# Gates' stage of a decoder block: low parts of weights on VectorE, a new order of its first products, and attention's results added up in DRAM by DMA

## The chip, the cores and the metric

One core of one Trainium2 chip runs the whole layer in one launch. The metric is the device time of one execution in microseconds (us); the time of a kernel is the median of its runs. Five engines have queues of their own: TensorE (PE, with its weight loads as PEld), VectorE (DVE), ScalarE (ACT), GpSimd (POOL) and SyncE (SP, which here only starts DMA transfers).

## What is computed

One decoder layer on 2048 tokens of width 1024, in float32. A projection gives pool channels, queries, keys, values and two gates; a causal pooling mixer and a sliding-window attention (window 128, 16 query heads of 64 on 2 key/value heads, a learned sink) run side by side; the gated sum goes through an output projection, and a convolutional gated MLP (width 2816) follows. Cut to what matters here:

```python
h = rmsnorm(x, attn_norm[l])
z = h @ w_in[l]                       # pool | q | k | v | gate_pool | gate_attn
gates = sigmoid(z[..., o4:] + b_gate[l])
g_pool, g_attn = gates[..., :D_MODEL], gates[..., D_MODEL:]
a = pool_mixer(u_pool, w_pool[l], pool_scale[l])
b = swa_sink_attention(q, k, v, sinks[l])
x = x + (g_pool * a + g_attn * b) @ w_out[l]
h = rmsnorm(x, ffn_norm[l])
up = causal_depthwise_conv(h @ w_up[l], conv_w[l], conv_b[l])
x = x + (silu(gate) * val) @ w_down[l]
```

## The kernel before

The tokens are worked in two chunks of 1024 (`T`). A float32 matrix product is made of three products of a reduced format: each operand is split into a high part (a copy in the reduced format) and a low part (operand less high part), and high·high, high·low and low·high are summed in PSUM. Weights therefore pass through a raw tile "R" (3 buffers) into a tile "U" (19 buffers) with both parts. `split` makes the low part by a subtraction on VectorE. `split_added` (L235 to L237) makes it without VectorE: ScalarE copies the high part (L235), ScalarE writes minus the high part into the low part (L236: the raw tile times −1, in the reduced format), and a DMA that GpSimd starts (L237) adds the raw tile to it in SBUF.

Each chunk goes through these stages: keys and values; attention; gates; output projection (`out_proj`); `up`; `down`. Attention is 32 items, 4 groups of heads (`q4` 3, 2, 1, 0) by 8 blocks of 128 queries. An item has `scores` (L863, then mask, maximum and exponentials on VectorE and ScalarE, L872 to L888), `probabilities` (transposes on TensorE, L896, and a select on GpSimd, L904) and `values` (L924). Between them TensorE runs `fillers`: products of the query, pool and gate projections that `fillers(c, group)` lists block by block. `values` copies each 64-partition half of its PSUM result to the other half of a tile (L934, ScalarE) and adds the two key/value halves (L935, VectorE) into a tile of 1 MB per group of heads; three of the four are stored into the DRAM tensor `tad`, the fourth (`q4` 3) stays in SBUF for the gates of the columns 6 and 7, which are fillers.

The other six column tiles of the gates are the gates' stage: six units (`Gates`, columns 4, 5, 2, 3, 0, 1), each a two-by-two block product done with seven products of 12 matmuls of 128x512 (L1161): `one` (A11·B11), `two` (A12·B21), `three` (S2·T2), `four` (S1·T1), `five` (S3·T3), `six` (S4·B22) and `seven` (A22·T4). B are quarters of the normalized input, T sums of them (`right_t1` to `right_t4`, from input tiles loaded and scaled by `scaled_input`, L1386); A are quarters of the unit's weights, S sums of them (L373 to L385, VectorE) out of the two raw tiles `w_ga` and `w_gp`. Each unit's `Blocks.step` makes such a part and splits it: three tiles of 128x1024 a unit by `halved` (with `split_added` for the gates, by L356 and L357 for `up`). `kept` (L1179) copies a product from PSUM, L1191 to L1209 add products up, `value` and `gate` (L1354 to L1365) apply the sigmoids and multiply by what `Gates.fetch` loads from `tad` (attention) and `dd` (pooling).

`Stream` hands out weights in a fixed order: at each `get` the raw tiles of the next two entries are loaded, and the next entry is split ahead. Within each engine, a scheduler sets the order of the instructions; each engine's queue then runs in that order, waiting on semaphores.

Of the kernel before, what the change touches and what calls it, by code (L numbers as in the profile page):

```python
# [26 lines left out]
P = 128  # L27
D = 1024
S = 2048
T = 1024  # L30
# [45 lines left out]
class Stream:  # L76
# [61 lines left out]
def fillers(c, i):  # L138

    q = queries_of(0) + queries_of(1)  # L140
    g = gates_of(0)
    pu = [pooled_of(j) for j in range(4)]
    if i == 3:
        out = [[f] for f in g[6:] + pu[3] + [("one", 0, 0), ("two", 0, 0)]]
        out[4].insert(0, ("gates", 0, 0))
        return out
    fold = [("fold", j, 0) for j in FOLDS[FOLD_FIRST:] if c == 0 and i == 0]
    out = fold + (q[:4] + pu[0][2:] + q[4:6], q[6:] + pu[1][:2] + g[:2] + pu[1][2:],
                  pu[2][:2] + g[2:6] + pu[2][2:])[i]
    return [out[n * len(out) // NB:(n + 1) * len(out) // NB] for n in range(NB)]  # L150
# [13 lines left out]
def weight_order():  # L164
    out = []
    for c in range(NCH):
        if c > 0:
            out.append(("kv",))
        else:
            out += [("fold", j) for j in FOLDS[:FOLD_LEAD]]  # L170
        out += [(kind, j) for parts in first_fillers(c) for kind, j, n in parts if n == 0]
        for i in range(4):
            out += [(kind, j) for parts in fillers(c, i) for kind, j, h in parts
                    if h == 0 and kind not in ("one", "two")]
        out += [("gates", i) for i in range(1, len(UNITS))]
# [27 lines left out]
def block_kernel(ctx: ExitStack, tc: tile.TileContext, x, xT, pos, vec, qkn, w_poolT, w_pool, w_q, w_kv,  # L203
# [29 lines left out]
    def split_added(hi, lo, src):  # L233

        A.copy(hi, src)  # L235
        A.activation(lo, src, AF.Copy, scale=-1.0)  # L236
        G.dma_start(lo, src.bitcast(F32R), accum_op=ALU.add)  # L237
# [51 lines left out]
    def split_weights(key, raws):  # L289
        if key[0] in ("up", "gates"):  # L290
            return Blocks(raws, key[0] == "gates")
# [8 lines left out]
        for raw in raws:  # L300
# [4 lines left out]
            if key[0] in ("ga", "pg", "pu") or key[0] == "q" and key[1] < 4:  # L305
                split_added(hi, lo, raw)
# [26 lines left out]
    class Blocks:  # L333
# [6 lines left out]
        def __init__(self, raws, added=False):  # L340
            self.raws, self.w, self.at, self.added = raws, {}, 0, added
# [8 lines left out]
        def halved(self, first, second, raw):  # L350
            t = up_.tile([P, 2, 8, P], F32R, "U")
            self.tiles.append(t)
            if self.added:
                split_added(t[:, 0], t[:, 1], raw)
            else:
                A.copy(t[:, 0], raw)  # L356
                V.tensor_sub(t[:, 1], raw, t[:, 0].bitcast(F32))  # L357
# [478 lines left out]

    def load_queries(it):
# [73 lines left out]
    def values(it):  # L911
# [15 lines left out]
        ob = qp.tile([P, 2, P], F32, "Q")  # L927
        pe = pv.rearrange("p (c e) q -> p e c q", e=2)
        if it["q4"] not in it["ta"]:
            it["ta"][it["q4"]] = up_.tile([P, 2, T], F32, "U")  # L930
        tt = it["ta"][it["q4"]][:, :, n * P:(n + 1) * P]
        for e in range(2):
            own, other = slice(64 * e, 64 * e + 64), slice(64 - 64 * e, 128 - 64 * e)
            A.copy(ob[own], pe[other, e])  # L934
            V.tensor_add(tt[own], pe[own, e], ob[own])  # L935


    tad, dd, xd = (dp.tile([8, P, T], F32, n) for n in ("tad", "dd", "xd"))

    def pair_of(t, j):  # L940
        return t[2 * j:2 * j + 2].rearrange("k p t -> p k t")
# [395 lines left out]
    class Gates(Up):  # L1337


        def __init__(self, c, ct, b):  # L1340
            super().__init__(c, ct, b, None)

        def halo(self, m):
            return fp.tile([P, 2 + T], F32, "F")

# [34 lines left out]
    def scaled_input(c, j):  # L1380
# [3 lines left out]
             .rearrange("(k p) t -> p k t", p=P))  # L1384
        for k in range(2):
            A.activation(t[:, k], t[:, k], AF.Identity,  # L1386
                         scale=vc[:, V_AN + 2 * j + k:V_AN + 2 * j + k + 1])
        return t

    def gates(c, units, b, xg, last_probabilities, last_values):  # L1390
# [21 lines left out]
        u0.four()  # L1412
        right_t3(xg, b)
        u0.three()
        weights(1, 2)
        u1.four("a")
# [3 lines left out]
        u0.six()  # L1420
# [3 lines left out]
        u1.three()  # L1424
        u0.gate()
        weights(2, 2)
        u1.five()
# [184 lines left out]
    def mixer(c, hs, kvw):  # L1612
# [48 lines left out]
        def done(it):  # L1661
            values(it)
            if it["n"] == NB - 1 and it["q4"] < 3:
                load(pair_of(tad, it["q4"]), ta[it["q4"]])

        xg = []
        for i in range(len(items)):
# [4 lines left out]
            if i > 1:  # L1672
                done(items[i - 2])
# [9 lines left out]
            if units[0].w:  # L1683
                units[0].w.step(1)
            if i == len(items) - 2:
                run_later(9)
                xg = [scaled_input(c, j) for j in (0, 1)]
        done(items[-2])
        run_later(9)
        return gates(c, units, b, xg, lambda: probabilities(items[-1]), lambda: done(items[-1]))  # L1690
# [105 lines left out]
```

## Time and profile before

| | before |
|---|---|
| median of 3 runs | 2505.67 us (2501.68 to 2507.39) |
| profiled execution, its own time | 2498.63 us |
| its span | 2496.9 us |
| mean granted clock of TensorE | 0.989 |
| gates' stage of chunk 0 | 385 to 546 us |
| gates' stage of chunk 1 | 1608 to 1768 us |

The profile is one execution. Its rows name the line, the engine, the operation, and the tiles as output<-input with buffer numbers left out. A row "[1.67 <-POOL M L904]" says that the engine was idle for 1.67 us before this group, until line 904 on GpSimd had written a tile M. `U<-R` stands for the accumulating DMA of L237.

### The profile page before, as it was taken

To read this page: it belongs to the slowest core of one execution; us is meant where nothing else is said; L and a number is where in the kernel's file an instruction comes from. 1 tells how busy PE (TensorE), PEld (TensorE's weight loads), DVE (VectorE), ACT (ScalarE), POOL (GpSimd) and SP (SyncE) were. 2 spreads that over 40 slices of the span, in tenths; PEclk is the share of its full clock that TensorE was granted. 3 is DMA by queue.
4 is the path that set the end of the run, shared out by engine and by line. 5 is a ranking of instruction groups with operands and counts; after the bars stand their busy time and mean duration, and the time that the engine had idled before them with its cause. 6 is when DMAs were issued, how large, how long until landed. Compare 5 with 4: busy or idle time off the path is not lost.

```text
span 2496.9 us, 30624 instructions
## 1 busy us (share of the span) xinstructions
PE 2403.2 (96%) x11108; PEld 1977.8 (79%) x11108; DVE 1898.7 (76%) x2994; ACT 1254.9 (50%) x2279; POOL 204.1 (8%) x154
## 2 busy tenths in 40 slices
PE   8999997988999999999999999988999999999999
PEld 7877875767888888878888888766788888888887
DVE  8577877566887777799955878855669777779994
ACT  6556556554555555543522544654545455554432
POOL 0123221100000000000002131211000000000000
PEclk9999999999999999999999999999999999999999
DMA  9677666879432233455234454478662222227321
GB/s 349 199 233 216 212 194 176 208 221 325 173 101 76 81 122 101 139 198 196 92 143 151 146 173 143 151 181 219 224 228 84 94 76 77 95 74 278 127 77 51
DMA packets 161912, 399.74 MB, mean 160 GB/s; under 512 B 14433, under 2 KB 50785, under 8 KB 153825
## 3 DMA queue, kind: packets, MB, share of 16 engines
q1 hardware_dynamic: 153840, 370.33, 43.6%
q0 software_dynamic: 7488, 27.27, 6.0%
q8 instruction: 87, 1.43, 0.2%
q14 instruction: 65, 0.52, 0.1%
q10 hardware_dynamic: 432, 0.19, 0.0%
HBM read 255.78 MB, written 114.69 MB: 148 GB/s over the span
## 4 chain that ended last, share of the span: by engine, by line
PE 78%; DVE 7%; DMA 6%; ACT 4%; issue 4%; POOL 0%; SPq 0%; DVEq 0%; ACTq 0%; POOLq 0%
PE f L1161 20%; PE f L252 18%; PE t L1161 12%; PE a L1161 6%; PE f L1593 4%; PE a L1593 4%; PE s L1593 4%; PE t L1593 4%; DMA U<-R 2%; PE a L924 1%; PE s L863 1%; PE a L252 1%; ACT Q L882 1%; PE t L896 1%; DMA R<-w_gp 1%
## 5 line engine op out<-in xcount | busy, mean ns | idle before, releaser
L252 PE MATMUL f<-U,U 128*128 128x512 f32 (+1 forms) x2784 | 652.3, 390 | 13.7 <-ACT U L229 5.4
L252 PEld LDWEIGHTS f<-U,U 128*128 128x128 f32 x2784 | 511.0, 189 | 122.8 <-ACT U L229 7.2
L1161 PE MATMUL f<-U,U 128*128 128x512 f32 x1872 | 456.6, 395 | 18.1 <-ACT Q L1179 9.0
L1161 PEld LDWEIGHTS f<-U,U 128*128 128x128 f32 x1872 | 354.7, 191 | 101.0 <-ACT Q L1179 13.8
L1161 PE MATMUL t<-U,U 128*128 128x512 f32 x1392 | 339.4, 397 | 16.2 <-DMA U<-R 13.8
L1227 DVE SCALAR_TENSOR_TENSOR M<-F,vc,M 128x1024 f32<-128x1024 f32 x176 | 225.2, 1282 | 140.8 <-ACT M L1224 140.5
L1161 PEld LDWEIGHTS t<-U,U 128*128 128x128 f32 x1392 | 265.2, 191 | 77.0 <-DMA U<-R 16.3
L1161 PE MATMUL a<-U,U 128*128 128x512 f32 x768 | 187.3, 390 | 2.9 <-DMA U<-R 2.9
L1161 PEld LDWEIGHTS a<-U,U 128*128 128x128 f32 x768 | 143.7, 188 | 33.6 <-DMA U<-R 3.7
L356 ACT CAST U<-R 128x1024 fp32r<-128x1024 f32 x120 | 125.4, 1053 | 62.6 <-DVE R L385 31.1
L1161 PE MATMUL f<-U,M 128*128 128x512 f32 x624 | 151.5, 390 | 2.1 <-DVE F L1205 2.1
L357 DVE TENSOR_TENSOR U<-R,U 128x1024 fp32r<-128x1024 f32 x120 | 146.5, 1222 | 0.0
L882 ACT ACTIVATE Q<-s,st,rq 128x128 f32<-128x128 f32 x256 | 114.0, 455 | 60.8 <-DVE st L879 58.6
L1161 PEld LDWEIGHTS f<-U,M 128*128 128x128 f32 x624 | 116.7, 188 | 27.9 <-DVE F L1205 3.6
L1213 ACT COPY F<-f 128x512 f32<-128x512 f32 x52 | 30.5, 587 | 189.7 <-PE f L1161 189.7
L1551 ACT CAST U<-U 128x1024 fp32r<-128x1024 f32 x76 | 79.0, 1051 | 84.4 <-PE s L1593 21.5
L904 POOL TENSOR_SCALAR_AFFINE_SELECT M<-M 128x1024 fp32r<-128x1024 f32 x64 | 93.6, 1463 | 334.3 <-DVE st L884 205.5
L1224 ACT ACTIVATE M<-F,vc 128x1024 f32<-128x1024 f32 x88 | 109.4, 1243 | 2.0 <-DVE F L1209 0.5
L1552 DVE TENSOR_TENSOR U<-U,U 128x1024 fp32r<-128x1024 f32 x76 | 92.0, 1219 | 3.9 <-ACT U L1551 3.8
L1551 ACT CAST F<-U 128x1024 fp32r<-128x1024 f32 x44 | 46.2, 1050 | 92.0 <-PE a L1593 53.7
L1179 ACT COPY Q<-f 128x512 f32<-128x512 f32 x104 | 61.0, 586 | 51.0 <-PE f L1161 50.9
L924 PE MATMUL a<-M,U 128*128 128x512 f32 x240 | 73.2, 411 | 13.4 <-POOL M L904 5.3
(281 smaller groups left out, 3877.8 us busy)
## 6 DMA issues: line engine op xcount, KB each, us to landing
R<-w_up SPq DMA_DIRECT2D x80, 512.0 KB, 3.8
U<-R POOLq DMA_DIRECT2D x52, 512.0 KB, 5.4
actd<-M SPq DMA_DIRECT2D x44, 512.0 KB, 2.7
U<-w_down SPq DMA_DIRECT2D x88, 256.0 KB, 5.2
U<-actd SPq DMA_DIRECT2D x88, 256.0 KB, 5.3
qd<-U SPq DMA_DIRECT2D x64, 256.0 KB, 3.8
Q<-qd SPq DMA_DIRECT2D x64, 256.0 KB, 4.1
R<-w_out SPq DMA_DIRECT2D x32, 512.0 KB, 5.0
```

The lines of the kernel that those rows point to most:

```text
L252: nc.tensor.matmul(out, a, b, start=(i == 0), stop=(i == n - 1))
L356: A.copy(t[:, 0], raw)
L357: V.tensor_sub(t[:, 1], raw, t[:, 0].bitcast(F32))
L882: A.activation(pr[:, h, :], sc[:, h, 0:P], AF.Exp, bias=nm[:, h:h + 1], scale=it["rq"][:, h:h + 1], accum_out=rs[:, h:h + 1])
L904: G.affine_select(own.rearrange("p a h q -> p (a h) q"), pa.bitcast(F32).rearrange("p a h q -> p (a h) q"), pattern=[[0, 8], [1, P]], base ...
L924: nc.tensor.matmul(pv, v, p[:, a], start=(i == 0), stop=(i == 2 * len(todo) - 1))
L1161: nc.tensor.matmul(bank, a[:, x, k, :], b[k // 2][:, y, k % 2, :], start=(first and i == 0), stop=(i == 11), skip_group_check=True)
L1224: A.activation(y, u[:, 2:], AF.Identity, bias=cw[:, 3, m:m + 1], scale=cw[:, 2, m:m + 1])
L1227: V.scalar_tensor_tensor(y, u[:, j:j + T], cw[:, j, m:m + 1], y, op0=ALU.mult, op1=ALU.add)
L1551: A.copy(hi, src)
L1552: V.tensor_sub(lo, src, hi.bitcast(F32))
L1593: nc.tensor.matmul(into[m], u[:, 0, c_], v[:, 1], start=(first and j == 0), stop=(k == n - 1 and j == 2), skip_group_check=True)
```

## The change

1. `halved` splits the gates' weights as those of `up`: a copy on ScalarE and a subtraction on VectorE. 36 uses of `split_added` go; 16 remain (queries, pool and gate projections), and their DMA now reads the weights in DRAM instead of the raw tile in SBUF.
2. `values` copies the whole PSUM result (128x512) once into a tile of 4 blocks. After every fourth block SyncE stores the first 64 partitions into `tad`, and GpSimd starts a DMA that adds the other 64 partitions to it in DRAM. For `q4` 3 the sum is loaded back (1 MB).
3. Fillers of the last group of heads: block 6 gets `one` and `two` of unit 0, block 7 those of unit 1 (before: unit 0's one after the other in blocks 6 and 7; unit 1's after attention). The weights of units 0 and 1 and the first input tiles are fetched, split and scaled at stated blocks.
4. In `gates`, `two` of unit 2, `four` of unit 0 and its S4·B22 (a new `early`; `six` then only adds) stand ahead of the sums T2, and unit 1's likewise ahead of T3.
5. At the gates' last entry the stream doesn't split the first `w_out` entry ahead; it is split together with the second at the end of `gates`.

```diff
-        if later is None:
+        if key[0] == "gates" and self.entries[i + 1][0] == "out":
+            pass
+        elif later is None:
             self.part(i + 2)
...
-        out = [[f] for f in g[6:] + pu[3] + [("one", 0, 0), ("two", 0, 0)]]
-        out[4].insert(0, ("gates", 0, 0))
-        return out
+        out = [[f] for f in g[6:] + pu[3]]
+        out[3].insert(0, ("gates", 0, 0))
+        out[5].insert(0, ("gates", 1, 0))
+        return out + [[("one", i, 0), ("two", i, 0)] for i in range(2)]
...
-    def split_added(hi, lo, src):
+    def split_added(hi, lo, src, again):
         A.copy(hi, src)
         A.activation(lo, src, AF.Copy, scale=-1.0)
-        G.dma_start(lo, src.bitcast(F32R), accum_op=ALU.add)
+        G.dma_start(lo, again.bitcast(F32R), accum_op=ALU.add)
...
-            if self.added:
-                split_added(t[:, 0], t[:, 1], raw)
-            else:
-                A.copy(t[:, 0], raw)
-                V.tensor_sub(t[:, 1], raw, t[:, 0].bitcast(F32))
+            A.copy(t[:, 0], raw)
+            V.tensor_sub(t[:, 1], raw, t[:, 0].bitcast(F32))
...
-        for e in range(2):
-            own, other = slice(64 * e, 64 * e + 64), slice(64 - 64 * e, 128 - 64 * e)
-            A.copy(ob[own], pe[other, e])
-            V.tensor_add(tt[own], pe[own, e], ob[own])
+        key = it["q4"], n // 4
+        if n % 4 == 0:
+            it["ta"][key] = up_.tile([P, 4, 512], F32, "U")
+        t = it["ta"][key]
+        A.copy(t[:, :, n % 4 * P:n % 4 * P + P], pv)
+        if n % 4 == 3:
+            c_ = slice(n // 4 * 512, n // 4 * 512 + 512)
+            dst = tad[2 * key[0]:2 * key[0] + 2, :, c_].rearrange("c (e d) t -> d (c e) t", e=2)
+            load(dst, t[0:64])
+            G.dma_start(dst, t[64:P], accum_op=ALU.add)
+            if key == (3, 1):
+                it["ta"][3] = up_.tile([P, 2, T], F32, "U")
+                load(it["ta"][3], pair_of(tad, 3))
...
+        def early(self):
+            self.mul(self.z, "S4", "B22")
+            self.z_done = True
...
         u0, u1, u2 = units[:3]
-        weights(1, 1)
-        u1.one()
+        weights(2, 1)
+        u2.one("t")
         last_probabilities()
         weights(1, 1)
-        u1.two()
-        weights(2, 1)
-        right_t1(xg, b, None)
-        u2.one("t")
+        u2.two()
         last_values()
-        xg += [scaled_input(c, j) for j in (2, 3)]
-        u2.two()
+        xg += [load_input(c, j) for j in (2, 3)]
+        u0.four()
+        u0.early()
+        weights(1, 2)
+        for j in (2, 3):
+            scale_input(xg[j], j)
         t2s = right_t2(xg, b, None)
-        u0.four()
+        u1.four("a")
+        u1.early()
         right_t3(xg, b)
         u0.three()
-        weights(1, 2)
-        u1.four("a")
+        u0.six()
         u0.five()
...
+            if group == 3:
+                if 3 <= n < 7:
+                    units[0].w.step(1)
+                if n == 5:
+                    run_later(9)
+                    units[1].w.step(1)
+                    xg.append(load_input(c, 0))
+                if n == 6:
+                    scale_input(xg[0], 0)
+                    xg.append(load_input(c, 1))
+                if n == 7:
+                    scale_input(xg[1], 1)
...
+        right_t1(xg, b, None)
```

TensorE's order at the end of attention in chunk 0, before the change. `a_... <-M` of L924 are values of a block, `t_... <-identr` of L896 its transposes; of the L1161 products, `f_4155` and `a_4185` are `one` and `two` of unit 1, `t_4216` and `a_4250` those of unit 2, `t_4274` is `four` of unit 0:

```order
L896 MATMUL t_4170<-identr_91,Q_4086 128x128 x4
L1161 MATMUL f_4155<-U_353,U_4150 128x512 x2
L1161 MATMUL a_4185<-U_363,U_4150 128x512 x2
L924 MATMUL a_4231<-M_4175,U_452 128x512 x2
L924 MATMUL a_4231<-M_4178,U_453 128x512 x2
L1161 MATMUL f_4155<-U_353,U_4150 128x512 x4
L1161 MATMUL f_4155<-U_358,U_4150 128x512 x6
L1161 MATMUL a_4185<-U_363,U_4150 128x512 x4
L1161 MATMUL a_4185<-U_368,U_4150 128x512 x6
L1161 MATMUL t_4216<-U_353,U_4203 128x512 x2
L1161 MATMUL t_4274<-U_4208,U_4132 128x512 x4
```

And the same place after it (lines moved by 3 to 5). `t_4090` and `a_4120` are `one` and `two` of unit 2, `t_4146` is `four` of unit 0 and then its S4·B22 (the rows with U_888 and U_893), while `a_4195`, next below these rows, the same of unit 1:

```order
L929 MATMUL a_4068<-M_4050,U_453 128x512 x2
L1164 MATMUL t_4090<-U_353,U_4086 128x512 x4
L1164 MATMUL t_4090<-U_358,U_4086 128x512 x6
L901 MATMUL t_4105<-identr_91,Q_4010 128x128 x4
L1164 MATMUL a_4120<-U_363,U_4086 128x512 x6
L1164 MATMUL a_4120<-U_368,U_4086 128x512 x6
L929 MATMUL a_4134<-M_4110,U_452 128x512 x2
L929 MATMUL a_4134<-M_4113,U_453 128x512 x2
L1164 MATMUL t_4146<-U_4075,U_3990 128x512 x6
L1164 MATMUL t_4146<-U_4079,U_3990 128x512 x6
L1164 MATMUL t_4146<-U_888,U_3990 128x512 x6
L1164 MATMUL t_4146<-U_893,U_3990 128x512 x6
```

Unit 1's `one` and `two` now stand before these rows, between scores, transposes and values of the last blocks, and 48 products without T2 to T4 follow the last values.

GpSimd's order in chunk 0 after the change, over about two groups of four blocks (L909 is the select, L240 the DMA of `split_added`, L941 the adding DMA of `values`):

```order
L909 AFFINE_SELECT M_3254<-M_3251 128x1024
L941 DMA tad_208<-U_3003 64x4x512
L909 AFFINE_SELECT M_3324<-M_3321 128x1024
L240 DMA U_3389<-w_gp 128x1024
L240 DMA U_3545<-wfold_84 128x1024
L909 AFFINE_SELECT M_3401<-M_3398 128x1024
L909 AFFINE_SELECT M_3472<-M_3469 128x1024
L909 AFFINE_SELECT M_3560<-M_3557 128x1024
L941 DMA tad_208<-U_3313 64x4x512
```

Each L941 stands between the selects of two blocks, behind the store of the same tile on SyncE's queue; before the change there were only selects and the DMAs of L237.

More of the change, by code (lines that the diff above doesn't have):

```diff
@@ L174, in weight_order @@
                     if h == 0 and kind not in ("one", "two")]
-        out += [("gates", i) for i in range(1, len(UNITS))]
+        out += [("gates", i) for i in range(2, len(UNITS))]
         out += [("out", m) for n in range(2) for m in range(KT)]
@@ L835, in rotate, with pair_of @@
         V.tensor_add(x[h, 1], x[h, 1], t[h, 0])
+    tad, dd, xd = (dp.tile([8, P, T], F32, n) for n in ("tad", "dd", "xd"))
+    def pair_of(t, j):
+        return t[2 * j:2 * j + 2].rearrange("k p t -> p k t")
     def load_queries(it):
@@ L1423, in gates @@
         weights(2, 1)
-        u1.three()
+        u1.six()
+        u1.five()
         u0.gate()
-        weights(2, 2)
-        u1.five()
+        weights(2, 1)
         n = len(units)
```

47 lines of the change are left out of this document (20 added, 27 removed).

## The prediction

> **What bounds the kernel now.** I read the page first, then busy times by stage, then TensorE's idle places in the gates' stage, then the waits there. The page's first part:
>
> ```profile
> span 2496.9 us, 30624 instructions
> PE 2403.2 (96%) x11108; PEld 1977.8 (79%) x11108; DVE 1898.7 (76%) x2994; ACT 1254.9 (50%) x2279; POOL 204.1 (8%) x154
> ```
>
> TensorE (PE) is busy 96% of the span; 2496.9 − 2403.2 = 93.7 us are idle. Its products are the same in number before and after, so the change can win only that idle time and what slow clock costs. Busy times by stage (start:end, length, then busy of PE, PEld, DVE, ACT, POOL, then granted clock, DMA share, GB/s):
>
> ```profile
> 130.00:385.00 255.00, 241.93 (x1225) 201.25 (x1224) 205.76 (x441) 142.44 (x414) 65.93 (x46) 0.99 0.71 213
> 385.00:546.00 161.00, 133.48 (x538) 102.40 (x537) 99.39 (x127) 89.99 (x126) 19.48 (x20) 0.94 0.71 192
> 546.00:660.00 114.00, 106.70 (x473) 85.99 (x472) 79.28 (x107) 57.26 (x90) 2.44 (x2) 0.99 0.83 295
> 1060.00:1284.00 224.00, 222.06 (x974) 181.60 (x973) 201.14 (x284) 93.94 (x112) 0.00 (x0) 1.00 0.48 164
> 1348.00:1608.00 260.00, 258.56 (x1341) 218.23 (x1341) 208.51 (x432) 119.97 (x392) 66.29 (x34) 1.00 0.47 157
> 1608.00:1768.00 160.00, 134.60 (x539) 103.34 (x538) 98.81 (x125) 89.52 (x127) 19.26 (x20) 0.94 0.71 191
> ```
>
> The second and the last rows are the gates' stage of the two chunks. TensorE is idle there for 27.5 and 25.4 us, 53 of the 94 us, and no engine is full: VectorE (DVE) has 99 of 161 us. The clock is 0.94 against 1.00 elsewhere; 6% of 161 us is about 9.7 us a chunk. So idle time and clock hold 37 and 35 us, **72 us in all, the most that the stage can give**. Attention in chunk 1 (row 1348) has 1.4 us idle in 260, so what the change saves there on other engines is hidden. Attention in chunk 0 has 13 us idle and out_proj (row 546) 7 us.
>
> The idle places of chunk 0 in TensorE's timeline (start, length, group, idle before it and what ended it):
>
> ```profile
> 391.09 0.73 PE L924 MATMUL a<-M,U 128*128 128x512 f32 x2 [1.67 <-POOL M L904]
> 394.24 0.63 PE L896 MATMUL t<-identr,Q 128*128 128x128 f32 x4 [1.47 <-DVE Q L888]
> 400.06 1.20 PE L924 MATMUL a<-M,U 128*128 128x512 f32 x4 [2.36 <-DVE F L1191]
> 404.72 0.50 PE L924 MATMUL a<-M,U 128*128 128x512 f32 x1 [1.15 <-ACT M L898]
> 407.00 1.22 PE L924 MATMUL a<-M,U 128*128 128x512 f32 x2 [1.05 <-POOL M L904]
> 410.20 3.91 PE L1161 MATMUL f<-U,U 128*128 128x512 f32 x10 [1.99 <-DMA U<-R]
> 419.95 2.56 PE L1161 MATMUL t<-U,U 128*128 128x512 f32 x10 [1.75 <-DMA U<-R]
> 429.21 0.50 PE L1161 MATMUL f<-U,U 128*128 128x512 f32 x1 [2.39 <-ACT U L1036]
> 445.16 2.57 PE L1161 MATMUL a<-U,U 128*128 128x512 f32 x10 [1.48 <-DMA U<-R]
> 456.21 1.43 PE L1161 MATMUL t<-U,U 128*128 128x512 f32 x5 [1.00 <-DMA U<-R]
> 471.08 2.88 PE L1161 MATMUL a<-U,U 128*128 128x512 f32 x12
> 473.80 2.88 PE L1161 MATMUL t<-U,M 128*128 128x512 f32 x12
> 509.02 7.17 PE L1161 MATMUL f<-U,U 128*128 128x512 f32 x24 [3.61 <-ACT Q L1179]
> 527.66 7.59 PE L1161 MATMUL t<-U,U 128*128 128x512 f32 x22 [4.31 <-DMA U<-R]
> ```
>
> Three kinds. **Attention's tail**, 388 to 410: the five quoted gaps are 7.7 us (the window's unquoted gaps are under 1 us each). **Waits for a low part that comes by accumulating DMA** (`U<-R`): 1.99 + 1.75 + 1.48 + 1.00 + 4.31 = 10.5 us, and the 3.61 us at 509 stand behind such a transfer in the chain of waits, as does the last gap:
>
> ```profile
> 505.98 5.05 DMA U<-R
> 519.41 8.20 DMA U<-R
> ```
>
> **The input's split**, 2.39 us at 429 and some gaps near 1 us. Twelve products back to back take 473.80 − 471.08 = 2.72 us, 0.227 each; at 527 twenty-two take 7.59, 0.345 each: the slow clock after a long gap.
>
> **Part 1: low parts on VectorE.** What a step costs now and then:
>
> ```profile
> L357 DVE TENSOR_TENSOR U<-R,U 128x1024 fp32r<-128x1024 f32 x120 | 146.5, 1222 | 0.0
> L236 ACT ACTIVATE U<-R 128x1024 fp32r<-128x1024 f32 x52 | 55.0, 1058 | 0.1
> L237 POOL DMA_DIRECT2D U<-R x52 | 45.4, 873 | 275.5 <-ACT U L236 113.2 <-DVE U L1037 43.0 <-DVE R L377 29.8
> U<-R POOLq DMA_DIRECT2D x52, 512.0 KB, 5.4
> POOL U L237 <- ACT U L236: 35.5, 8, 10.9
> ```
>
> Of 52 steps, 36 (6 units, 3 tiles, 2 chunks) are the gates'. Each loses 1.06 us of ScalarE, 0.87 of GpSimd (POOL) and 5.4 of transfer behind the cast, 7.3 us of latency, and gets one subtraction of 1.22 us. VectorE takes on 36 × 1.22 = 44 us, 18 subtractions a chunk; four of them now run inside attention, 14 × 1.22 = 17 us in the stage. 99 + 17 = 116 us of VectorE against some 122 of products (538 × 0.227). Six units share them, 19.4 us each, and a unit's 84 products take 19.0. Row 1060 shows VectorE at 201 of 224 us, 90%, with TensorE at 99%, so this can be carried if the order is kind; 116/0.9 = 129 us. I count all ten-odd microseconds of `U<-R` gaps and the 3.6 behind one as gone: **−14 us a chunk**. What is late next is the raw weights on which the sums are formed, and VectorE itself. The wait that remains, in the stage of chunk 0:
>
> ```profile
> DVE R L376 <- DMA R<-w_gp: 9.8, 2, 5.7
> ```
>
> Up to 5.7 us at once, hidden behind products now. With no slack on VectorE some of it leaks: I take **+3 us**, between 0 and 9.8, nearer to 0 because the stage's first part, attention's last blocks and the input's sums, holds more than its share of the 116.
>
> **Part 2: order.** The last two blocks of attention carried 12 products each beside them (2.7 us, the row at 471); now 24 each, and right after it 24 products of S1·T1 with S4·B22, which need only two tiles of the input's T1 and one of B22, are followed by 24 of the next unit's. Some 30 us of products lie ahead of the first that needs T4, and by adding durations in the new order VectorE has about as much to do in that time. Attention's tail shrinks but doesn't vanish: two blocks gain 2 × 2.7 us of cover against 7.7 us of gaps: **−5 us**. The 2.4 us at 429 and the like are partly covered: **−1.5**.
>
> New waits: the second input tile is loaded one block later and its scaling stands ahead of the last blocks' exponentials on ScalarE. Loads of this size and their neighbours, us to landing last:
>
> ```profile
> U<-xT SPq DMA_DIRECT2D x8, 1024.0 KB, 8.6
> tad<-U SPq DMA_DIRECT2D x6, 1024.0 KB, 4.9
> M<-tad SPq DMA_DIRECT2D x12, 512.0 KB, 6.2
> U<-made_ga SPq DMA_DIRECT2D x2, 1024.0 KB, 10.7
> ```
>
> An 8.6 us landing against a block of some 8 us leaves 2 to 3 us of ScalarE waiting, of which TensorE sees up to that: I take **+2.5** (0 to 8.6, the whole landing).
>
> **Part 3: out's first split later.** The first weight of out_proj is no longer split while the last gates run; the first two now come together at the stage's end: four casts and four subtractions of half the size of L357's, about 0.6 us each, 2.4 us on either engine, in front of out_proj's first product. By the order some 50 products, 11 us, cover them, so **+1** (0 to 4.8).
>
> **Part 4: results added in DRAM.** Per block two copies of 0.37 us and two additions of 0.42 go, one copy of 128x512 comes:
>
> ```profile
> L934 ACT COPY Q<-a 64x256 f32<-64x256 f32 x128 | 47.1, 368 | 50.0 <-DVE U L935 47.7
> L935 DVE TENSOR_TENSOR U<-a,Q 64x256 f32<-64x256 f32 x128 | 53.5, 418 | 28.3 <-ACT Q L934 26.0
> L1179 ACT COPY Q<-f 128x512 f32<-128x512 f32 x104 | 61.0, 586 | 51.0 <-PE f L1161 50.9
> ```
>
> ScalarE saves 0.74 − 0.59 = 0.15 us a block, VectorE 0.84, 53.5 us over 64 blocks. Attention hides nearly all of it (1.4 us idle in chunk 1); it pays for Part 1's 44 us in the sum of VectorE. In chunk 0 there are 13 idle us to win, by fewer accumulates into SBUF and raw buffers that come free sooner; I take **−2**, once (−13 to +10). The price: 16 stores and 16 accumulating DMAs of 512 KB for 6 stores of 1 MB, and two loads of 1 MB. Behind each accumulate, which must wait for its store, GpSimd's selects queue (the order above), and behind SyncE's load of the sums in chunk 1 `made_ga` queues. Nothing before accumulates in DRAM; a store of 1 MB lands in 4.9, an accumulate in 5.4. A block has 8 us between selects, so one is hidden where it comes out of step; I take **+1.5 a chunk**, from 0 to 8 × 4.9 = 39.
>
> **Clock.** Fewer gaps, less slow clock: of 9.7 us about 6.5 come back, by the share of the gaps that goes (about two thirds): **−6.5**.
>
> Sum a chunk: −14 − 5 − 1.5 − 6.5 + 3 + 2.5 + 1 + 1.5 = **−19**; twice that and the −2 of chunk 0 make −40. The profiled execution took 2498.6 us (span 2496.9 and 1.7 around it); it would become 2459. The median of the runs is 2505.7, 7 above it; taken off the median, **2466 us**.
>
> A rule is weighed here. Selects on GpSimd, alone and beside a VectorE operation:
>
> ```profile
> 248.90 2.03 POOL L904 TENSOR_SCALAR_AFFINE_SELECT M<-M 128x1024 fp32r<-128x1024 f32 x1 [8.04 <-DVE st L884]
> 257.52 1.08 POOL L904 TENSOR_SCALAR_AFFINE_SELECT M<-M 128x1024 fp32r<-128x1024 f32 x1 [5.77 <-DVE st L884]
> ```
>
> One is 0.95 us longer. By the Trainium skill, "SBUF — State Buffer", section "Who interferes with whom", a VectorE instruction with two SBUF inputs and a GpSimd instruction that reads SBUF exclude each other, which speaks against Part 1, as its subtractions read two tiles. The trace's 0.95 us agrees. By it the four subtractions a chunk that fall into attention would cost at most 8 × 0.95 = 8 us, −32 for −40; without it nothing. The sum goes without, as attention's selects have slack.
>
> **Rivals.**
> *VectorE becomes the bound.* For it: 116 us against 122 of products, chains in which each waits for the other. At 81% of its time (205.8 of 255 in chunk 0's attention) the stage takes 143 us, 18 less than now, −36; at 75%, 155, −12. Against it: row 1060's 90%. I put it at −20: 2486.
> *The stage runs nearly gapless.* All of the new waits hidden and 4 us left of 36 a chunk: −64, 2442. Against it: attention's last block, whose probabilities and values form one chain over four engines.
> *The accumulates hold attention up (slower).* Each of the 16 keeps GpSimd for a store's landing, 4.9 us, with a select behind it that the next values need. At 16 × 4.9 = 78 less the 40, +38: 2544. It decides from 40/16 = 2.5 us each not hidden. Against it: a block's 8 us and GpSimd busy only 66 of 255 us.
> *It moves the stalls only.* out_proj of chunk 0 has a DMA share of 0.83 and waits for weights now; arriving 20 us earlier it may wait that much longer, and chunk 1 likewise: 2501 to 2508.
>
> **How the numbers follow.** Forecast 0.50 (2453 to 2478), VectorE the bound 0.20 (2478 to 2500), gapless 0.15 (2434 to 2453), stalls moved 0.07, slower by accumulates 0.08. The range 2438 to 2499 leaves out a fifth of the gapless case, 0.03, a little of the second, 0.01, and the last two, 0.15. Within 0.2% (2500.7 to 2510.7, about what a measurement of this kernel can tell from no change) lie the moved stalls: 0.07; slower 0.08; faster 0.85.
>
> **What would show it.** Part 1: no `U<-R` gaps on TensorE in the stage, the stage at about 140 us, VectorE at 115 in it, clock 0.97 or more. Part 2: gaps between the last blocks of 4 us or less. Part 3: under 2 us idle at out_proj's start. Part 4: accumulates landing within 6 us, no select behind one that TensorE waits for. Wrong it would be if attention grew by more than 5 us in a chunk, or TensorE waited for VectorE's subtractions or for raw weights by more than 10.

## The result, and the profile after

| | before | after |
|---|---|---|
| median | 2503.68 us (4 runs, 2497.79 to 2507.39) | 2440.24 us (4 runs; three of them 2438.13 to 2440.7) |
| ratio | | 0.9746, 95% interval 0.972 to 0.9772 |
| profiled execution, its span | 2498.63, 2496.9 us | 2440.7, 2439.0 us |
| mean granted clock | 0.989 | 0.994 |

The change made the kernel 63 us faster by the medians, 58 by the two profiles (2498.6 and 2440.7). One of the four runs after took 3567.56 us, at a granted clock of 0.619; it counts in that median and in nothing else here. The first part of the page after:

```profile
span 2439.0 us, 30309 instructions
PE 2383.8 (98%) x11108; PEld 1973.2 (81%) x11108; DVE 1888.0 (77%) x2902; ACT 1205.1 (49%) x2179; POOL 192.3 (8%) x134
```

TensorE's idle time is 55 us in place of 94, and its busy time, for the same 11108 instructions, 19 us less. The granted clock rose with it, from 0.989 to 0.994 as a mean over the span, which by itself would be some 12 of the 19 us. To see where the time went I cut both kernels at the same three events in TensorE's timeline: the first scores of a chunk, the first scores of its last group of heads (for short, the last group), and the first product of out_proj. Out_proj's own stretch is counted from there to the transposes of L635 in the norm that follows; 20 us of its products come after them, in both kernels. Busy times by these stretches, before (chunk 0 twice, then chunk 1; columns as in the prediction):

```profile
130.00:337.00 207.00, 193.93 (x976) 160.43 (x975) 164.15 (x351) 117.05 (x334) 55.88 (x38) 0.98 0.74 222
337.00:546.00 209.00, 181.48 (x787) 143.22 (x786) 141.00 (x216) 115.38 (x205) 29.53 (x28) 0.95 0.68 188
1366.00:1558.40 192.40, 190.96 (x993) 160.96 (x992) 162.12 (x337) 93.18 (x309) 45.27 (x25) 1.00 0.44 149
1558.40:1767.60 209.20, 183.80 (x798) 145.21 (x798) 140.32 (x210) 113.58 (x204) 29.41 (x27) 0.95 0.66 186
```

And after:

```profile
130.00:325.60 195.60, 190.63 (x975) 159.56 (x974) 148.83 (x307) 110.90 (x312) 61.04 (x43) 0.99 0.88 243
325.60:509.80 184.20, 173.79 (x787) 140.99 (x786) 150.18 (x212) 95.73 (x176) 18.41 (x13) 0.98 0.61 184
1332.20:1524.50 192.30, 190.64 (x991) 160.92 (x990) 146.25 (x293) 87.23 (x287) 50.94 (x30) 1.00 0.61 180
1524.50:1708.20 183.70, 174.47 (x797) 142.74 (x796) 149.81 (x206) 93.89 (x174) 18.39 (x12) 0.98 0.51 158
```

Last group to out_proj: 209.2 to 184.2 and 209.1 to 183.7 us, −25 in each chunk. Attention up to the last group: −11 in chunk 0, nothing in chunk 1. Out_proj up to L635: 79.1 to 81.4 and 69.6 to 71.5 us, +2 each. That is −11 − 25 − 25.4 + 2.3 + 1.9 = −57.2 of the 57.9 us between the spans. The same three numbers are given below for each experiment.

TensorE's gaps after, last blocks and gates of chunk 0:

```profile
386.54 1.22 PE L868 MATMUL s<-U,Q 128*128 128x256 f32 x8 [2.19 <-ACT Q L887]
396.28 0.73 PE L929 MATMUL a<-M,U 128*128 128x512 f32 x2 [1.65 <-POOL M L909]
403.72 0.74 PE L929 MATMUL a<-M,U 128*128 128x512 f32 x2 [0.76 <-POOL M L909]
407.91 3.02 PE L1164 MATMUL t<-U,U 128*128 128x512 f32 x12 [0.68 <-ACT Q L1182]
412.34 2.56 PE L1164 MATMUL a<-U,U 128*128 128x512 f32 x10 [0.50 <-DVE U L357]
419.00 4.41 PE L1164 MATMUL a<-U,U 128*128 128x512 f32 x12 [2.51 <-ACT Q L1182]
506.97 3.02 PE L1164 MATMUL f<-U,M 128*128 128x512 f32 x12 [1.15 <-DVE F L1208]
```

No `U<-R` is left among them, and between 419 and 507 TensorE has no gap of over 0.15 us. The longest gap is 2.51 us at 419, behind a copy out of PSUM on ScalarE. The waits in the same place of chunk 1 tell why:

```profile
ACT U L1039 <- DMA tad<-U: 4.8, 1, 4.8
PE a L1164 <- ACT Q L1182: 2.8, 1, 2.8
...
1614.00:1624.00 10.00, 7.28 (x25) 5.78 (x26) 6.35 (x7) 4.63 (x6) 0.00 (x0) 0.83 0.23 90
```

(The letters PE, ACT and DMA name who waits for what; then us in all, times, longest. The last row has the columns of the stretches above.) ScalarE wants to write a split of the input (L1039) into the U buffer that the last attention results leave, and waits 4.8 us until their accumulate into `tad` has landed; the copy of PSUM stands behind it in ScalarE's order, and TensorE behind that. In the 10 us around this gap the granted clock is 0.83.

### The profile page after: what moved, and what is told of

It is laid out like the page before. It is cut to its first block, busy times and chain, and to the rows that moved or that the text cites. A ratio compares the mean times of both kernels' runs of the same rounds, so it can differ in the third digit from the quotient of the medians.

```text
span 2439.0 us, 30309 instructions
## 1 busy us (share of the span) xinstructions
PE 2383.8 (98%) x11108; PEld 1973.2 (81%) x11108; DVE 1888.0 (77%) x2902; ACT 1205.1 (49%) x2179; POOL 192.3 (8%) x134
## 4 chain that ended last, share of the span: by engine, by line
PE 51%; DMA 3%; DVE 2%; ACT 1%; issue 1%; POOL 0%; DVEq 0%; SPq 0%; ACTq 0%
PE f L255 11%; PE f L1164 10%; PE t L1164 5%; PE f L1614 4%; PE a L1614 4%; PE s L1614 4%; PE t L1614 4%; PE a L1164 3%; PE a L929 1%; PE a L255 1%; PE s L868 1%; PE t L901 0%; DMA M<-xd 0%; DMA F<-dd 0%; DMA U<-xT 0%
## 5 line engine op out<-in xcount | busy, mean ns | idle before, releaser
L1164 PE MATMUL f<-U,U 128*128 128x512 f32 x1872 | 447.6, 390 | 1.3 <-ACT Q L1182 1.3
L1164 PE MATMUL t<-U,U 128*128 128x512 f32 x1392 | 329.5, 391 | 2.1 <-ACT Q L1182 2.1
L356 ACT CAST U<-R 128x1024 fp32r<-128x1024 f32 x156 | 162.7, 1052 | 84.9 <-DVE R L377 46.5
L357 DVE TENSOR_TENSOR U<-R,U 128x1024 fp32r<-128x1024 f32 x156 | 190.2, 1220 | 1.2 <-ACT U L356 1.0
L909 POOL TENSOR_SCALAR_AFFINE_SELECT M<-M 128x1024 fp32r<-128x1024 f32 x64 | 97.6, 1525 | 333.0 <-DVE st L889 226.2
L936 ACT COPY U<-a 128x512 f32<-128x512 f32 x64 | 37.6, 587 | 101.5 <-PE a L929 101.3
```

The costliest lines, as they stand in the source:

```text
L909: G.affine_select(own.rearrange("p a h q -> p (a h) q"), pa.bitcast(F32).rearrange("p a h q -> p (a h) q"), pattern=[[0, 8], [1, P]], base ...
L1164: nc.tensor.matmul(bank, a[:, x, k, :], b[k // 2][:, y, k % 2, :], start=(first and i == 0), stop=(i == 11), skip_group_check=True)
```

## The experiments

Low parts, the DMA's source and the new values were each made alone on the kernel before; source, values and out's later split were each undone alone in the kernel after. The order was run without the rest (order_only), and its undoing together with that of source and split (vec_values). The ratio is to the kernel before as it was run beside each kernel (medians of 2499.9 to 2503.7 us). The numbers:

| kernel | first scores to last group, chunk 0 / 1 | last group to out_proj | out_proj | median us (range) | ratio to before, interval |
|---|---|---|---|---|---|
| before | 204.5 / 192.2 | 209.2 / 209.1 | 79.1 / 69.6 | 2503.7 (2497.8–2507.4) | |
| after | 193.5 / 192.3 | 184.2 / 183.7 | 81.4 / 71.5 | 2440.2 (2438.1–2440.7) | 0.9746 (0.972–0.9772) |
| only_vec | 207.9 / 192.2 | 182.0 / 183.2 | 78.6 / 69.8 | 2445.1 (2443.8–2448.1) | 0.9783 (0.9768–0.9797) |
| only_dram_src | 212.9 / 192.2 | 208.5 / 208.5 | 80.5 / 70.4 | 2507.5 (2504.7–2510.6) | 1.0032 (1.002–1.0043) |
| only_values | 192.7 / 192.3 | 223.6 / 223.5 | 78.8 / 69.5 | 2518.6 (2514.4–2523.2) | 1.0076 (1.0057–1.0094) |
| order_only | 204.6 / 192.3 | 211.9 / 209.3 | 79.1 / 69.9 | 2503.6 (2498.3–2508.5) | 1.0014 (1.0003–1.0025) |
| vec_values | 196.5 / 192.3 | 180.4 / 176.5 | 77.9 / 69.6 | 2427.9 (2426.5–2430.4) | 0.9713 (0.9699–0.9728) |
| no_values | 216.0 / 192.2 | 177.9 / 178.3 | 81.4 / 71.9 | 2446.4 (2444.9–2452.0) | 0.979 (0.9776–0.9805) |
| no_dram_src | 193.1 / 192.4 | 189.2 / 182.8 | 80.5 / 71.2 | 2441.9 (2435.1–2445.2) | 0.976 (0.974–0.9779) |
| out_ahead | 194.2 / 192.3 | 186.2 / 181.6 | 80.1 / 69.0 | 2436.1 (2434.2–2438.3) | 0.9745 (0.9731–0.976) |
| after_again | 194.4 / 192.0 | 187.3 / 185.5 | 81.7 / 70.7 | 2441.2 (2437.6–2446.7) | 0.9766 (0.9744–0.9788) |
| vec_values_again | 194.5 / 192.3 | 178.7 / 176.2 | 80.0 / 70.5 | 2427.9 (2426.5–2428.3) | 0.971 (0.9695–0.9725) |
| last_old | 194.7 / 192.4 | 178.4 / 178.4 | 80.8 / 71.3 | 2431.7 (2430.5–2432.2) | 0.9725 (0.971–0.9741) |
| last_twice | 195.1 / 193.0 | 182.6 / 182.0 | 81.1 / 72.6 | 2439.7 (2435.5–2441.3) | 0.9753 (0.9733–0.9774) |

The two profiles of the kernel after differ by 3.1 and 1.8 us from the last group to out_proj, so less than that isn't read from this column. Some expectations cut chunk 0 one block of attention later (212.3 and 201.4 us for 204.5 and 209.2); the differences that they name hold all the same.

### Low parts on VectorE alone (only_vec)

```diff
-            return Blocks(raws, key[0] == "gates")
+            return Blocks(raws, False)
```

> Before, with the gates' low parts on VectorE and nothing else changed. Theory V (the waits for accumulated low parts are the main loss): the U<-R gaps and the 3.6 us behind one go, with some of the slow clock; from the first scores of the last group of heads to out_proj's first product each chunk is 14 to 18 us shorter (201.4 in chunk 0 and 209.2 in chunk 1 before), the whole time 28 to 36 us less. Theory O (the order is the main thing; without it the waits only change their name): at most 8 us a chunk, 16 in all, with new gaps that end at VectorE's subtractions. Attention of chunk 0 up to the last group: unchanged within 2 us by both.

−27.2 and −25.9 us a chunk, far over theory O's 8 and well over theory V's 14 to 18: theory V, and its size too small. Chunk 0's attention up to the last group, which both theories had unchanged within 2 us, is 3.4 us longer. Its stretches from the last group to out_proj:

```profile
340.50:522.50 182.00, 173.69 (x787) 141.39 (x786) 160.16 (x234) 98.84 (x187) 15.39 (x10) 0.98 0.50 164
1534.00:1717.30 183.30, 174.52 (x799) 142.54 (x798) 159.43 (x228) 97.18 (x186) 15.44 (x9) 0.98 0.49 161
```

Idle time falls from 27.5 to 8.3 us in chunk 0, TensorE's busy time by 7.8, as the clock goes from 0.95 to 0.98. VectorE rises from 141 to 160 us of a shorter stretch, 88%, and few gaps end at it; ScalarE falls by 16.5. Its gaps of 0.5 us and more in the whole stretch are those of attention's last blocks and two for the input's split:

```profile
393.79 0.50 PE L924 MATMUL a<-M,U 128*128 128x512 f32 x1 [1.58 <-DVE M L901]
395.96 0.89 PE L924 MATMUL a<-M,U 128*128 128x512 f32 x2 [1.67 <-POOL M L904]
...
406.55 1.18 PE L924 MATMUL a<-M,U 128*128 128x512 f32 x2 [1.65 <-POOL M L904]
425.18 0.49 PE L1161 MATMUL f<-U,U 128*128 128x512 f32 x1 [1.77 <-ACT U L1036]
427.97 1.66 PE L1161 MATMUL f<-U,U 128*128 128x512 f32 x6 [0.65 <-DVE U L1037]
```

### The DMA's source in DRAM alone (only_dram_src), and undone (no_dram_src)

```diff
-        G.dma_start(lo, src.bitcast(F32R), accum_op=ALU.add)
+        G.dma_start(lo, again.bitcast(F32R), accum_op=ALU.add)
...
-                split_added(hi, lo, raw)
+                split_added(hi, lo, raw, slabs[key[0]][key[1]])
```

> Before, with the DMA of the 16 projection low parts reading the weights in DRAM and not the raw tile; the gates' own keep the raw tile as source. Theory S (chunk 0's attention gained its 11 us because a raw buffer comes free once ScalarE has read it, so that the next weights are loaded sooner): first scores to the last group's first scores, 212.3 us in chunk 0 before, becomes 200 to 204, the time 8 to 13 us less. Theory L (the gain is from the lighter values): 212 within 2 us, no change in time. Chunk 1 unchanged by both, as its projections' weights are kept from chunk 0.

> After with the raw tile as the source of the 16 projection low parts again. If the source in DRAM costs time by itself, as it did alone (8.4 us more in chunk 0's attention): up to the last group's first scores 185 to 192 for 193.5, the time 2 to 8 us less than the changed kernel. If it only costs beside the old values: 193.5 within 1.5, no change.

Theory S falls: the source in DRAM made chunk 0's attention 8.4 us longer, with a wait of 7.7 us for the low part of `w_ga` that comes by this DMA. Undone in the kernel after, it moves nothing there (193.1 for 193.5) nor in the time. So it costs beside the old values and neither costs nor gains beside the new ones.

### The new values alone (only_values), and undone (no_values)

The edit is part 2 of the change, that of `values`, by itself, in either direction.

> Before, with attention's results stored and added up in DRAM and nothing else changed. Theory L: chunk 0 up to the last group's first scores 212.3 becomes 200 to 204, the time 8 to 13 us less. Theory S: within 2 us. Rival H (accumulates hold GpSimd's selects up): longer, by up to 4.9 us at each of the 6 places up to there in a chunk, with waits of TensorE for the select; in chunk 1, where TensorE has no slack, it would show best. I expect chunk 1's 192.2 us of that stretch unchanged within 1 us.

> After with the old values (two copies and two additions a block, three stores of 1 MB a chunk). If the new values are what shortened chunk 0's attention: its stretch up to the last group's first scores is back at 204 to 210 (193.5 in the changed kernel), chunk 1's 192.3 unchanged, the stretch to out_proj 181 to 184 as with the low parts alone, the time 10 to 16 us over the changed kernel. If the gain hangs on the DMA's source in DRAM in company with the rest: 193 to 196 still, no change in time.

Theory L holds for chunk 0's attention: −11.8 us alone, and undone in the kernel after +22.5. Beside the old values the source in DRAM costs 8.4 of these and the low parts on VectorE 3.4 (only_vec), which leaves some 11 for the values in this direction too. In chunk 0 up to the last group, TensorE's idle time falls from 13.1 to 4.3 us with the new values alone. The longest of its gaps before, and a wait that stands ahead of it:

```profile
318.70 2.08 PE L863 MATMUL s<-U,Q 128*128 128x256 f32 x8 [3.84 <-ACT Q L882]
...
ACT U L235 <- DMA R<-wfold: 4.2, 1, 4.2
```

ScalarE waited for a raw weight, with copies of the values and exponentials behind the cast in its order, and TensorE for those. With the new values alone neither the gap nor the wait is there; with the low parts alone both still are.

no_values missed in the other stretch: 177.9 and 178.3 us to out_proj, not 181 to 184, so that it is only 6 us over the kernel after. In the new order the new values cost 6.3 and 5.4 us a chunk there (more under the buffer, below).

Rival H is not seen up to the last group: chunk 1's 192.3 us is unchanged to 0.1 us in both directions, with 6 stores and accumulates there. But no theory had +14.4 us a chunk from the last group on. The stretches of only_values in chunk 0, and the gaps in question:

```profile
130.00:325.00 195.00, 190.67 (x975) 159.81 (x974) 148.74 (x306) 110.92 (x312) 61.20 (x43) 0.99 0.88 243
325.00:548.60 223.60, 187.29 (x787) 145.74 (x786) 133.68 (x197) 112.40 (x195) 33.03 (x31) 0.92 0.72 198
```

```profile
388.17 0.79 PE L929 MATMUL a<-M,U 128*128 128x512 f32 x1 [4.13 <-ACT M L903]
393.10 0.80 PE L929 MATMUL a<-M,U 128*128 128x512 f32 x1 [4.14 <-DVE M L906]
...
417.76 3.80 PE L1164 MATMUL t<-U,U 128*128 128x512 f32 x10 [4.09 <-DMA U<-R]
...
510.38 7.60 PE L1164 MATMUL f<-U,U 128*128 128x512 f32 x24 [4.94 <-ACT Q L1182]
```

The order of this kernel puts four scalings of the input (L1389, 1.1 us each) on ScalarE between the exponentials of one of the last blocks, and the gaps that end at accumulated low parts are 13.6 us in chunk 0, for 10.5 before. In all, TensorE's idle time grows by 8.8 us and its busy time by 5.8, at a clock of 0.92 for 0.95. With the low parts on VectorE, in the old order, the loss is gone (vec_values, below). There the four scalings stand ahead of a block's exponentials too, and no gap is over 2.5 us: the scalings alone are not the cause.

### The order alone (order_only)

The kernel after, with low parts by DMA from the raw tile, the old values and out's first weight split ahead. What it keeps of the change is the order, cut here to:

```diff
+        return out + [[("one", i, 0), ("two", i, 0)] for i in range(2)]
...
+        u0.four()
+        u0.early()
```

> After, with low parts by accumulating DMA again, the raw tile as their source, the old values, and out's first weight split ahead: what is left of the change is the order (fillers of the last group, the gates' first products). Theory O: most of the 25 us a chunk from the last group's first scores to out_proj is here, 15 us a chunk or more, 30 in all. Theory V: 5 to 8 us a chunk, with U<-R gaps of 8 us or more a chunk left on TensorE. If the two parts only work together, both this and the kernel with low parts alone give under 8.

+2.7 and +0.2 us: the order alone gains nothing; theory O is out, and theory V's 5 to 8 us for the order did not come either. The gaps move: its low parts are waited for 4.24 us (at 430.57) and 3.58 (at 454.72) in one go. "Only together" isn't it either, since low parts alone gave 26.

### Low parts and new values in the old order (vec_values, vec_values_again, after_again)

The edits of only_vec and only_values together; after_again is the kernel after, unchanged.

> Before with low parts on VectorE and results added up in DRAM, in the old order and with out's first weight split ahead. Parts that simply add up: chunk 0 from the first scores to the last group's first scores 192.7 as with the values alone, from there to out_proj 182 to 183 in each chunk as with the low parts alone, span 2432 to 2438, below the changed kernel's 2439. If instead the new values cost 14 us a chunk in the last blocks and the gates in any old order (as they did alone, 223.6 against 209.2), and the new order is what avoids it: 194 to 198 a chunk from the last group's first scores on, span 2458 to 2466.

> Low parts on VectorE and results added in DRAM, in the old order, once more. If the new order, the DRAM source and out's later split cost together what the stages of the two profiles say (7 and 3.8 us from the last group to out_proj, 3.5 and 1.9 in out_proj, against 3 won in chunk 0's attention): 11 to 14 us under the changed kernel. If the difference was one of the batches: within 5.

> The changed kernel once more, beside the next one on the same chip: 2438 to 2442, 58 to 62 us under before.

The parts add up, and better than that: from the last group to out_proj 180.4 and 176.5 us. Chunk 0 up to the last group falls short: 196.5 us, and 194.5 in the second profile, for the 192.7 expected.

```profile
328.90:509.20 180.30, 173.14 (x787) 139.65 (x786) 153.73 (x215) 95.73 (x177) 20.35 (x13) 0.99 0.63 193
1520.10:1696.60 176.50, 172.54 (x798) 140.21 (x797) 153.60 (x208) 94.05 (x176) 18.83 (x12) 1.00 0.55 168
```

Side by side on one chip it takes 2427.85 us, the kernel after 2441.15, and no run of the one reaches the range of the other: **this kernel beats both, and the rest of the change, order, source and later split together, costs 13 us.** In this pair's profiles it does so from the last group to out_proj, 8.6 and 9.3 us, and a little in out_proj; they show 18 us in all, as the profiled run of the kernel after was the slowest of its four.

### Out's first split ahead again (out_ahead)

```diff
-        if key[0] == "gates" and self.entries[i + 1][0] == "out":
-            pass
-        elif later is None:
+        if later is None:
```

> After with out's first weight split ahead again, at the gates' last entry. My sum had 1 us a chunk for the later split; the profile of after has out_proj 2.3 and 1.9 us longer, with gaps that end at the cast of w_out. If the later split is their cause: out_proj's stretch 79.1 and 69.6 us as before (81.4 and 71.5 after), the time 3 to 4 us less, the gates' stage unchanged. If the split ahead holds a raw buffer back from the last gates' weights: out_proj shorter but the gates' stage longer by 2 us or more a chunk, no change or slower.

Out_proj is 1.3 and 2.5 us shorter, the median 4 to 5 us under the two of the kernel after, ranges barely touching; the differences from the last group to out_proj have both signs and are about what two profiles of one kernel differ by. So the later split seems to cost some 2 us a chunk, as the first expectation has it. It is not clear of noise: the two profiles of vec_values differ by 2.1 us in chunk 0's out_proj, and by the ratios, each to the kernel before beside it, out_ahead stands at 0.9745 and the kernel after at 0.9746 and 0.9766. What is left in chunk 0's out_proj is its weights, 3 us and more at once in either kernel, after:

```profile
522.12 11.52 PE L255 MATMUL f<-U,U 128*128 128x512 f32 x48 [1.01 <-ACT U L232]
535.10 6.09 PE L255 MATMUL f<-U,U 128*128 128x512 f32 x24 [1.45 <-ACT U L232]
544.54 0.92 PE L255 MATMUL f<-U,U 128*128 128x512 f32 x2 [3.35 <-ACT U L232]
```

### The buffer behind the last results (last_old, last_twice)

last_old has the old values for the last group of heads alone; last_twice adds the second half of the last four blocks' results twice:

```diff
+        if it["q4"] == 0:
...
+            if n == NB - 1:
+                load(pair_of(tad, 0), it["ta"][0])
+            return
```

```diff
             G.dma_start(dst, t[64:P], accum_op=ALU.add)
+            if key == (0, 1):
+                G.dma_start(dst, t[64:P], accum_op=ALU.add)
```

> After, with the old values for the last group of heads alone, so that no accumulate follows the last block. Theory U: in the new order a split of the input (the first of T3) takes the U buffer that the last results leave, and ScalarE waits 4.8 us for their accumulate to land, with the copies of PSUM behind it, for which TensorE waits 2.5 and 2.8 us. Then here that wait and the slow clock after it are gone: the stretch from the last group's first scores to out_proj 179 to 181.5 for 184.2 and 183.7, the time 5 to 9 us under the changed kernel. Rival: the new order itself is what costs, buffers or not: 183 or more, within 2 us of the changed kernel.

> After, with the second half of the last four blocks' results added twice in DRAM, so that the columns of group 0 come out of another sum. Theory U: the U buffer is held for one more accumulate, 8 us or so; ScalarE's wait for it grows from 4.8 to 11 to 14 us, TensorE's stall behind it from 2.8 to 8 to 12, the stretch to 190 to 196 in each chunk, the time 12 to 24 us over the changed kernel. Rival: no one waits for that landing; within 3 us of the changed kernel, with at most the load of the sums for the gates a little later.

last_old goes as theory U says and a little further: 9.4 us under the kernel after, run beside it, and 3.9 over vec_values. Its two stretches from the last group to out_proj:

```profile
326.90:505.40 178.50, 172.33 (x788) 139.95 (x787) 156.30 (x230) 98.42 (x184) 17.47 (x11) 0.99 0.58 184
1520.30:1698.70 178.40, 171.72 (x798) 140.25 (x797) 155.75 (x223) 96.78 (x183) 13.97 (x10) 1.00 0.49 157
```

So 9.4 of the 13 us that the rest of the change costs are gone when the last group keeps the old values; no_values, where all groups keep them, has the same stretches (177.9 and 178.3).

last_twice missed: no longer, but 182 to 183 us, and the time within 1.5 us of the kernel after, as the rival has it. In its program the extra DMA moved the buffers round: the buffer behind the last results falls to a cast of a gate's weights, not to the input's split. GpSimd's DMAs and the wait, chunk 1:

```profile
1606.86 1.02 POOL L941 DMA_DIRECT2D tad<-U  x1 [6.38 <-ACT U L356]
1614.94 1.01 POOL L943 DMA_DIRECT2D tad<-U  x1 [7.06 <-DMA tad<-U]
```

```profile
ACT U L356 <- DMA tad<-U: 3.7, 1, 3.7
```

The second accumulate starts 8 us after the first, and ScalarE waits 3.7 us for it. TensorE's gaps of 2.5 and 2.8 us behind the copy of PSUM are gone, but another stands in each chunk some 8 us later, 1.36 us in chunk 0 and 2.23 in chunk 1. The row in chunk 1, and pieces of the chain that leads to it:

```profile
1624.59 4.53 PE L1166 MATMUL f<-U,M 128*128 128x512 f32 x12 [2.23 <-DVE F L1210]
...
1614.94 6.54 DMA tad<-U
1621.63 1.05 ACT U L356
1623.85 0.69 DVE F L1210
```

The late cast holds up its subtraction on VectorE, a sum (L1210) stands behind that in VectorE's order, and TensorE waits for the sum. So the dose was not the one that I meant, and the two kernels show this much: the late landing reaches TensorE by way of whatever the buffer goes to, and going back to the old values for the last group is worth 5 to 9 us a chunk from there to out_proj, by the two profiles of the kernel after. That the buffer is all of that isn't shown: the gap itself is 2.5 to 2.8 us and the slow clock behind it; last_old's last blocks also run in another order, without the waits for selects.

## Why the prediction was right, and where it was off

The direction and the range held, 2438 to 2499 for 2440.2, 2 us inside its lower edge. The forecast itself did not: it had −40 us and 2453 to 2478, and the profiles give −57.9. The range held by luck, as it took in most of the 2434 to 2453 of the rival of a nearly gapless stage. The time lies there, but not by that mechanism: the stage kept 10.4 and 9.2 idle us from the last group on, and of the 57.9 us that the profiles give 11 came in attention, which that rival didn't have.

Of the signs that the prediction named, the `U<-R` gaps are gone and the clock is 0.98; the gaps of the last blocks (5.3 us for 4 or less) and the accumulates' landing (7.7 us for 6) missed. Two waits after, between 375 and 540, on which the next points draw:

```profile
ACT U L1406 <- DMA U<-xT: 4.5, 1, 4.5
...
DVE R L376 <- DMA R<-w_gp: 1.1, 2, 0.6
```

- **Part 1, low parts on VectorE** (−14 of gaps, +3 of raw weights, −6.5 of clock, −17.5 a chunk): right in mechanism, mis-sized. Alone it gives −27.2 and −25.9: −19.2 of idle time and −7.8 of busy time in chunk 0. I counted the gaps whose row names `U<-R` and the 3.61 us behind one, 14 in all; the other 5 of the 19 are two gaps behind ScalarE's copies and a sum (0.92 and 0.97) and 3.1 us of attention's tail. The step also takes 16.5 us of work from ScalarE, which may be why these went; no run separates that. The +3 for raw weights did not come: VectorE's wait for them is 1.1 us (the second row), ScalarE's 2.6, and no gap of TensorE ends there. VectorE as the bound, the 0.20 rival, did not come either: 88% of the stretch with low parts alone.
- **Part 2, the order** (−5 −1.5): wrong. Alone +2.7 and +0.2; beside the rest it is part of what costs 13 us. The step that failed is "two blocks gain 2 × 2.7 us of cover". From the last group to the last values TensorE was idle for 8.7 and 8.0 us before and for 8.5 and 8.3 with the order alone: other waits took the place of those for selects, 3.77 us for a low part's negative on ScalarE (L236) and 2.47 for an addition of `values` among them. Where the low parts are on VectorE this idle time is smaller, but not by the order: 5.6 and 5.8 us with low parts alone, 4.8 and 1.6 with the new values beside them, 5.6 and 3.6 in the kernel after. Of the 5.3 us of gaps from 386 to 408 after, 2.19 are the input tile's (next point) and 2.4 end at selects. The input's split, 2.4 us at 429 before, is no longer waited for, but the 2.51 us behind the copy of PSUM stand in its place. Beside the old values the new order seems to help (177.9 and 178.3 for 182.0 and 183.2 in only_vec, where out's split and the source differ too).
- **The input tile loaded later** (+2.5): chunk 0's 2.19 us at 386, behind ScalarE's wait for a tile of the input (the first row above); 0.77 us at its place in chunk 1. Right in place, and in size in chunk 0.
- **Part 3, out's split** (+1): some 2 a chunk, not clear of noise.
- **Part 4, results in DRAM**. The −2 for chunk 0's attention was mis-sized: −11, and the new values are what does it. +1.5 a chunk for accumulates between selects: nothing up to the last group, where chunk 1 would show it. What I didn't see is the accumulate's hold on its source's buffer. The upper bound of 39 us a chunk for the queue on GpSimd was far off the mark, the rival at 2544 with it.
- **Selects beside VectorE**: I left their longer time out of the sum. A select's mean went from 1463 to 1525 ns, 4 us over 64 of them. Attention before the last group is unchanged to 0.1 us in chunk 1; the four subtractions themselves fall into the last group, where selects of 2.03 us stand before two of TensorE's waits (1.66 us at 1592 after; before has the like, 1.67 at 391). No run separates that part.

Left open: which of the new values' differences, shorter work on two engines, stores of half the size, or the order that follows, shortens chunk 0's attention; its engines, its DMA and its order change together. Of the 13 us, 9.4 need the new values of the last group together with the rest, and the split seems to be about 4; the source costs nothing beside the new values. The order was not undone alone in the kernel after.

## What to carry to other kernels

A step taken off an in-order engine can be worth more than the gaps that carry its name, here 19 us of idle time and 8 of slower products in chunk 0, for gaps of 14: look at what stood behind it on that engine too. A change made of several parts is taken apart before it is kept: one line gave 55 us by itself, one part 17 more on top of it, and what was done beside them gave 13 back. And the buffer that an accumulating DMA read came free here only when it had landed (ScalarE waited 4.8 us for it), so ask what is put there next, and who stands behind that.

## What was unexpected of the hardware

DMAs of 512 KB that GpSimd starts, medians to landing: after,

```profile
tad<-U POOLq DMA_DIRECT2D x16, 512.0 KB, 7.7
U<-wfold POOLq DMA_DIRECT2D x8, 512.0 KB, 8.6
```

and with low parts alone, the 16 that remain with an SBUF source,

```profile
U<-R POOLq DMA_DIRECT2D x16, 512.0 KB, 7.9
```

and, in no_dram_src, where both kinds have an SBUF source,

```profile
U<-R POOLq DMA_DIRECT2D x16, 512.0 KB, 6.4
tad<-U POOLq DMA_DIRECT2D x16, 512.0 KB, 8.3
```

A plain store of the same results lands in 4.4. The 5.4 us that I took from before as an accumulate's landing was the median of 52, in which the gates' 36 were the quicker; in chunk 0's attention the low parts took 8.3 before. With the new values they took 6.0 there from the raw tile (no_dram_src) and, by weight, 7.4 to 9.7 from DRAM (after). Accumulates into `tad` took 7.6 there and 8.4 in chunk 1's attention after, where the DMA engines are less busy (0.88 and 0.61). What sets these times no run shows.
